# Padding in SBUF in a two-block fp32 kernel: where the tiles begin

## The chip, the cores and the metric

The kernel runs on one core of a Trainium2 chip. The metric is the device time of one launch in microseconds (us), the median of three runs. Nothing runs on the host but a re-layout of the inputs before the launch.

## The reference, cut to what matters

Two transformer blocks follow each other on 256 tokens of width 1024, all in float32. The first block has a SwiGLU feed-forward layer, a mixer and a second SwiGLU layer, the second block the same on 256 tokens plus 256 context tokens, with a modulation computed from a conditioning vector.

```python
def first_block(x, ...):
    x = x + 0.5 * swiglu(rmsnorm(x, ffn1_norm), w_gate, w_up, w_down)      # 1024 -> 2816 -> 1024
    x = x + hybrid_mixer(rmsnorm(x, mix_norm), w_in, ...)                  # gated linear attention and a short convolution
    x = x + 0.5 * swiglu(rmsnorm(x, ffn2_norm), ...)
    return rmsnorm(x, final_norm)

def second_block(x, c, ctx, ...):
    h, hc = x + grid_pos_emb(rows), ctx
    mods, mods_c = silu(c) @ w_ada + b_ada, silu(c_ctx) @ w_ada + b_ada    # nine vectors each
    h  = ffn_sublayer(h,  mods[0:3],   g_ffn1, w_ffn1_in, w_ffn1_out)
    hc = ffn_sublayer(hc, mods_c[0:3], g_ffn1, w_ffn1_in, w_ffn1_out)
    # mLSTM over both directions, a spatial gating branch, a merge and an output projection
    ...
    h  = ffn_sublayer(h, mods[6:9], g_ffn2, w_ffn2_in, w_ffn2_out)
    return rmsnorm_2(h, g_final)
```

## The kernel before, in words

Tokens are held in tiles of 128; a tile of activations is transposed by TensorE into XH and XL, so that the channel stands on the partitions. Almost every product of the kernel is done in three matmuls of type float32r: each fp32 operand is split into a rounded high part and the remainder (`split_out`: ScalarE copies the high part, VectorE subtracts it), and `mm3` or `mm3r` add high x high, high x low and low x high in one PSUM bank.

A weight comes as a unit of 128 x 1024 fp32 (512 KB): `load` issues its DMA on SyncE into one of 4 `raw` buffers, `split` writes it into one of 5 `wh` and one of 5 `wl` buffers. A matmul `mm(out, l, r)` loads `l` into the array (the stationary operand, an LDWEIGHTS of 128 columns) and streams `r` through it (the moving operand). In the profile's names, `acc<-wh,XH` is a matmul with moving wh and stationary XH.

- `proj_chunk` (gate and up layers of the two-token feed-forward layers, mixer projections): stationary XH or XL, moving wh or wl, 512 columns.
- `projT2` (gate and up layers of the second block): the other way round, stationary wh or wl, moving XH or XL, 512 columns for four token tiles and 256 for two.
- The down layers in `ffn2tok` and `ffn4tok`: stationary the hidden activations (high part hh, low part hl), moving wh or wl, 512 columns. The hidden tiles are taken by `salloc` from 18 shared buffers S0 to S17, the one that was freed longest ago first.

In `ffn4tok`, the first part of the down layer has six units for each half d of the output. A unit is 24 matmuls: two values of q, four token tiles, three products. In the built program the hidden pairs (hh, hl) of the six units stand in (S3, S4), (S7, S5), (S13, S14), (S16, S17), (S8, S9) and (S10, S11), the same for both values of d. With FFN4's first chunk, in `proj_chunk`, eight weight tiles that were split ahead into slots are the moving operands: (S1, S12), (S3, S11), (S2, S8), (S4, S7), for two token tiles one after the other, six matmuls for each pair and token tile.

The order of the work on each engine is that of the program text. SBUF is laid out pool by pool in the order of the pools in `body` and, within a pool, in the order in which tags first appear, each buffer rounded up to 32 bytes: const (with ident, mhalf, tri, XH, XL and others), xres, small, tmp, bc, rp, slots, raw, wsp. What stands where is therefore the running sum of the sizes before it. `salloc` asks for shapes up to 4096 bytes of the partition, and for two shapes of 4 x 258 elements (4128 bytes).

Of the kernel before, what the change touches and what calls it, by code (L numbers as in the profile page):

```python
# [9 lines left out]
F32 = mybir.dt.float32  # L10
F32R = mybir.dt.float32r
# [3 lines left out]
P = 128  # L15
D = 1024
# [7 lines left out]
class Kern:  # L24
# [26 lines left out]
    def psum(self, tag, shape):  # L51
        return self.ps.tile(shape, F32, tag=tag, name=self.nm(tag), bufs=4)

    def salloc(self, shape, dt=F32):
        i = self.free_slots.pop(0)
        t = self.slots.tile(shape, dt, tag=f"S{i}", name=self.nm(f"S{i}"))
        self.slot_of[id(t)] = (i, t)
        return t

# [1044 lines left out]
    def run(self):  # L1104
        nc, A = self.nc, self.A
        x = {}
        for t in (2, 3):
            x[t] = self.xres.tile([P, D], F32, tag=f"x{t}", name=f"x{t}")
        self.ident = self.cpool.tile([P, P], F32, tag="ident", name="ident")
        make_identity(nc, self.ident)  # L1110
        g = {"f1": self.bc.tile([P, D], F32, tag="bc", name="bc_f1")}
        pre = []
# [5 lines left out]
        self.mhalf = self.cpool.tile([P, 4], F32, tag="mhalf", name="mhalf")  # L1118
        nc.gpsimd.memset(self.mhalf, -0.5)
        self.tri = self.cpool.tile([P, 2, P], F32, tag="tri", name="tri")  # L1120
        self.XH = self.cpool.tile([P, 8, 512], F32R, tag="XH", name="XH")
        self.XL = self.cpool.tile([P, 8, 512], F32R, tag="XL", name="XL")
        lat = (2, 3)

        def res_half(t, d, ps):
# [173 lines left out]
def body(tc, A, out):  # L1299
    with tc.tile_pool(name="const", bufs=1) as cpool, \  # L1300
            tc.tile_pool(name="xres", bufs=1) as xres, \
            tc.tile_pool(name="small", bufs=16) as small, \
            tc.tile_pool(name="tmp", bufs=6) as tmp, \
            tc.tile_pool(name="bc", bufs=4) as bc, \
            tc.tile_pool(name="rp", bufs=2) as rp, \
            tc.tile_pool(name="slots", bufs=1) as slots, \
            tc.tile_pool(name="raw", bufs=4) as raw, \
            tc.tile_pool(name="wsp", bufs=5) as wsp, \
            tc.tile_pool(name="dram", bufs=1, space=bass.MemoryType.DRAM) as dram, \
            tc.tile_pool(name="ps", bufs=1, space=bass.MemoryType.PSUM) as ps:  # L1310
        pools = dict(cpool=cpool, xres=xres, small=small, tmp=tmp, bc=bc, rp=rp, slots=slots, raw=raw, wsp=wsp, ps=ps)
        k = Kern(tc, A, out, pools)
        k.modd = dram.tile([112, P], F32, tag="modd", name="modd")
        k.mrow = dram.tile([36, 256], F32, tag="mrow", name="mrow")
        k.run()
# [129 lines left out]
```

## Time and profile before

| | us |
|---|---|
| median of 3 runs | 1427.51 (1427.47 to 1428.04) |
| profiled execution, its own time | 1426.11 |
| its span, first to last instruction | 1424.3 |
| PE (matmuls) busy | 1404.2 (99%), 7222 instructions |
| PEld (weight loads) busy | 1170.0 (82%) |
| DVE (VectorE) busy | 919.5 (65%) |
| ACT (ScalarE) busy | 626.5 (44%) |

The granted clock of TensorE is 0.998 of full speed over the span. Matmuls are pipelined and the ends of their records are modelled, so a record's duration (393 ns and more for 512 columns) overlaps the next; what a matmul costs is the distance from its start to the next one's start. A distance is read from the timeline (start times of rows and the number of matmuls between them) or from a window, whose busy time is divided by the matmuls that start in it. A window's count has up to four more than that, since records that reach over its edges are counted too.

### The profile page before, as it was taken

What the parts mean: (1) busy time and instruction counts of PE and PEld (TensorE: products, weight loads), DVE (VectorE), ACT (ScalarE), POOL (GpSimd) and SP (SyncE); (2) the same over time, 40 slices, a digit from 0 to 9 for tenths busy, and PEclk for the clock granted to TensorE, in tenths of its full rate; (3) what the DMA queues carried; (4) which work ended last, traced back from release to release, by engine and by line L of the source; (5) the groups of instructions that cost most, each with busy time, mean ns of one, the idle gap of its engine ahead of it and who ended that gap; (6) DMA issues with size and microseconds to landing.
All of it is one profiled execution on the core that took longest, in us unless ns stands there. A gap on an engine that the chain in (4) does not pass through costs nothing. (4 is left out here: it accounts for less than half of the span.)

```text
span 1424.3 us, 18795 instructions
## 1 busy us (share of the span) xinstructions
PE 1404.2 (99%) x7222; PEld 1170.0 (82%) x7222; DVE 919.5 (65%) x1308; ACT 626.5 (44%) x914; POOL 29.3 (2%) x49
## 2 busy tenths in 40 slices
PE   7999999999999999999999999999999999999997
PEld 5888788778888898888888887888988887899986
DVE  5998556878988475542555446476886566655545
ACT  5445447464446442322122224343865455444442
POOL 0000000000000000000000001001010000000000
PEclk9999999999999999999999999999999999999999
DMA  8888646457887664643565442333335666465662
GB/s 278 307 269 275 205 136 204 134 166 259 290 275 254 203 210 132 195 147 102 191 209 178 147 148 94 115 104 129 102 104 187 198 192 206 142 197 179 184 207 69
DMA packets 73307, 260.71 MB, mean 183 GB/s; under 512 B 8172, under 2 KB 9216, under 8 KB 73216
## 3 DMA queue, kind: packets, MB, share of 16 engines
q1 hardware_dynamic: 72928, 259.11, 56.3%
q8 instruction: 57, 0.93, 0.3%
q10 hardware_dynamic: 288, 0.39, 0.1%
q14 instruction: 34, 0.28, 0.1%
HBM read 258.32 MB, written 1.14 MB: 182 GB/s over the span
## 5 line engine op out<-in xcount | busy, mean ns | idle before, releaser
L69 DVE TENSOR_TENSOR wl<-raw,wh 128x1024 fp32r<-128x1024 f32 (+1 forms) x381 | 459.0, 1212 | 330.3 <-ACT wh L66 326.7
L66 ACT ACTIVATE wh<-raw 128x1024 fp32r<-128x1024 f32 (+1 forms) x381 | 398.3, 1049 | 609.0 <-PE acc L79 457.9
L79 PE MATMUL acc<-wh,XH 128*128 128x512 f32 (+2 forms) x816 | 277.3, 398 | 0.4 <-ACT t L66 0.4
L79 PE MATMUL acc<-wh,XL 128*128 128x512 f32 (+2 forms) x816 | 273.4, 393 | 0.2 <-DVE XL L69 0.2
L79 PE MATMUL acc<-wl,XH 128*128 128x512 f32 (+2 forms) x816 | 272.4, 392 | 0.0
L79 PE MATMUL acc<-wh,S 128*128 128x512 f32 x872 | 237.1, 394 | 0.4 <-DVE t L72 0.4
L79 PE MATMUL acc<-XH,wh 128*128 128x512 f32 (+1 forms) x776 | 201.5, 339 | 0.0
L79 PE MATMUL acc<-XH,wl 128*128 128x512 f32 (+1 forms) x776 | 201.2, 339 | 0.0
L79 PE MATMUL acc<-XL,wh 128*128 128x512 f32 (+1 forms) x776 | 201.1, 339 | 0.0
L79 PEld LDWEIGHTS acc<-wh,S 128*128 128x128 f32 x872 | 162.8, 188 | 38.8 <-DVE t L72 1.1
L543 DVE SCALAR_TENSOR_TENSOR S<-raw,S 128x1024 f32<-128x1024 f32 x112 | 136.9, 1222 | 70.6 <-DMA raw<-in_w_ada 69.9
L79 PEld LDWEIGHTS acc<-wh,XL 128*128 128x128 f32 x816 | 152.2, 189 | 34.6 <-DVE XL L69 1.1
L79 PEld LDWEIGHTS acc<-wl,XH 128*128 128x128 f32 x816 | 152.0, 188 | 33.7 <-DVE wl L69 0.3
L79 PEld LDWEIGHTS acc<-wh,XH 128*128 128x128 f32 x816 | 151.7, 189 | 33.9 <-ACT t L66 0.6
L79 PEld LDWEIGHTS acc<-XL,wh 128*128 128x128 f32 x776 | 133.0, 188 | 17.5
L79 PEld LDWEIGHTS acc<-XH,wl 128*128 128x128 f32 x776 | 132.9, 188 | 17.5
L79 PEld LDWEIGHTS acc<-XH,wh 128*128 128x128 f32 x776 | 132.9, 188 | 17.5
L79 PE MATMUL acc<-wl,S 128*128 128x512 f32 x436 | 133.0, 393 | 0.0
L79 PEld LDWEIGHTS acc<-wl,S 128*128 128x128 f32 x436 | 81.9, 188 | 18.4
L66 ACT ACTIVATE S<-t 128x512 fp32r<-128x512 f32 (+2 forms) x58 | 31.4, 542 | 30.2 <-DVE t L69 30.2
L66 ACT ACTIVATE XH<-tr 128x512 fp32r<-128x512 f32 x44 | 26.0, 596 | 41.8 <-PE tr L152 41.3
L152 PE MATMUL tr<-ident,t 128*128 128x128 f32 x200 | 32.1, 285 | 10.4 <-DVE t L69 9.6
(165 smaller groups left out, 892.9 us busy)
## 6 DMA issues: line engine op xcount, KB each, us to landing
raw<-in_gu SPq DMA_DIRECT2D x176, 512.0 KB, 4.4
raw<-in_d SPq DMA_DIRECT2D x88, 512.0 KB, 4.3
raw<-in_w_ada SPq DMA_DIRECT2D x72, 512.0 KB, 4.5
raw<-in_w_in SPq DMA_DIRECT2D x68, 512.0 KB, 4.3
raw<-in_w_qk SPq DMA_DIRECT2D x16, 512.0 KB, 3.5
bc<-modd SPq DMA_DIRECT2D x10, 512.0 KB, 4.4
raw<-in_w_out SPq DMA_DIRECT2D x8, 512.0 KB, 3.5
raw<-in_w_b SPq DMA_DIRECT2D x8, 512.0 KB, 4.3
```

The lines of the kernel that those rows point to most:

```text
L66: return self.nc.scalar.activation(out=out, in_=in_, func=func, **kw)
L69: return self.nc.vector.tensor_tensor(out=out, in0=a, in1=b, op=op)
L79: self.nc.tensor.matmul(out, l, r, start=start, stop=stop, **kw)
L152: self.nc.tensor.transpose(tr[:, j, :], src[:, j * P:(j + 1) * P], self.ident)
L543: nc.vector.scalar_tensor_tensor(out=junk, in0=raw, scalar=1.0, in1=cb[r], op0=ALU.mult, op1=ALU.mult, accum_out=mc[:, o:o + 1])
```

## The change

One tile of 96 elements and one of 32 are added in the const pool and one of 96 in the rp pool; nothing writes or reads them. XH and XL move up in the const pool to stand right behind ident. `salloc` asks for 1152 elements in place of 4 x 258 and hands out the first 1032 of them in the old shape (the row of a head stays 258 elements, the buffer becomes 4608 bytes).

The instructions of all engines, their order and their waits are the same in both programs; apart from the row length of the 4 x 258 tiles only start addresses differ. In the built programs the starts within the partition, in bytes modulo 512, are:

```
                         before                          after
ident                    128                             0
XH, XL                   160                             0
x, tmp (t), bc           0                               0
S0 / S1                  128 / 160                       0 / 0
S2, S3                   192                             0
S4 to S7                 224                             0
S8 to S12                256                             0
S13 to S17               288                             0
raw, wh, wl              288                             0
tri                      160                             32
cst, mc, cols            160, 288, 224                   160, 288, 224
```

The pieces that the matmuls take from these tiles lie at multiples of 512 bytes from their starts, except in the 4 x 258 tiles, whose heads follow each other at 1032 bytes.

```diff
--- before.py
+++ after.py
+    def pad(self, pool, n):
+
+        pool.tile([P, n], F32, tag=f"pad{n}", name=self.nm("pad"), bufs=1)
+
     def salloc(self, shape, dt=F32):
         i = self.free_slots.pop(0)
-        t = self.slots.tile(shape, dt, tag=f"S{i}", name=self.nm(f"S{i}"))
+        if len(shape) == 3 and shape[1] * shape[2] > D:
+            t = self.slots.tile([P, D + P], dt, tag=f"S{i}", name=self.nm(f"S{i}"))
+            t = t[:, :shape[1] * shape[2]].rearrange("p (a b) -> p a b", a=shape[1])
+        else:
+            t = self.slots.tile(shape, dt, tag=f"S{i}", name=self.nm(f"S{i}"))
         self.slot_of[id(t)] = (i, t)
         return t
...
+        self.pad(self.cpool, 96)
         self.ident = self.cpool.tile([P, P], F32, tag="ident", name="ident")
+        self.XH = self.cpool.tile([P, 8, 512], F32R, tag="XH", name="XH")
+        self.XL = self.cpool.tile([P, 8, 512], F32R, tag="XL", name="XL")
...
         self.tri = self.cpool.tile([P, 2, P], F32, tag="tri", name="tri")
-        self.XH = self.cpool.tile([P, 8, 512], F32R, tag="XH", name="XH")
-        self.XL = self.cpool.tile([P, 8, 512], F32R, tag="XL", name="XL")
+        self.pad(self.cpool, 32)
...
         k = Kern(tc, A, out, pools)
+        k.pad(rp, 96)
```

## Rows read from the trace of the kernel before

**Rows 1.** Page, part 1: busy us, share of the span, instructions.
```profile
PE 1404.2 (99%) x7222; PEld 1170.0 (82%) x7222; DVE 919.5 (65%) x1308; ACT 626.5 (44%) x914; POOL 29.3 (2%) x49
```
**Rows 2.** Waits of PE, the longest: us in total, times, longest us.
```profile
PE tr L152 <- DVE t L69: 9.6, 3, 6.4
```
**Rows 3.** Groups by form, matmuls and a weight load: count, busy us, mean ns.
```profile
L79 PE MATMUL acc<-wh,XH 128*128 128x512 f32 x784 | 271.3, 402 | 0.4 <-ACT t L66 0.4
...
L79 PE MATMUL acc<-wh,S 128*128 128x512 f32 x872 | 237.1, 394 | 0.4 <-DVE t L72 0.4
L79 PEld LDWEIGHTS acc<-wh,S 128*128 128x128 f32 x872 | 162.8, 188 | 38.8 <-DVE t L72 1.1 <-ACT t L66 0.7 <-DVE t L69 0.5
...
L79 PE MATMUL acc<-wl,S 128*128 128x512 f32 x436 | 133.0, 393 | 0.0
...
L79 PE MATMUL acc<-XH,wh 128*128 128x512 f32 x392 | 123.8, 395 | 0.0
...
L79 PE MATMUL acc<-XH,wh 128*128 128x256 f32 x384 | 77.7, 282 | 0.0
```
**Rows 4.** Timeline of PE, ffn4tok's down layer, first rows of units: start, us, what.
```profile
652.45 2.00 PE L79 MATMUL acc<-wh,S 128*128 128x512 f32 x8
...
657.95 2.00 PE L79 MATMUL acc<-wh,S 128*128 128x512 f32 x8
...
663.41 1.98 PE L79 MATMUL acc<-wh,S 128*128 128x512 f32 x8
...
668.86 2.03 PE L79 MATMUL acc<-wh,S 128*128 128x512 f32 x8
...
674.46 0.39 PE L79 MATMUL acc<-wh,S 128*128 128x512 f32 x1
...
702.14 2.03 PE L79 MATMUL acc<-wh,S 128*128 128x512 f32 x8
...
707.74 0.39 PE L79 MATMUL acc<-wh,S 128*128 128x512 f32 x1
```
**Rows 5.** Windows, PE: us, busy (count), PEclk, DMA share, GB/s; XH with wh.
```profile
46.28:57.55 11.27, 11.27 (x52) 1.00 0.93 337
...
579.78:646.79 67.01, 67.01 (x291) 1.00 0.48 155
713.33:825.32 111.99, 111.99 (x481) 1.00 0.53 172
1097.95:1155.90 57.95, 57.95 (x253) 1.00 0.61 196
```
**Rows 6.** Timeline of PE, FFN4's first chunk, moving operands in slots.
```profile
1237.49 0.63 PE L79 MATMUL acc<-S,XH 128*128 128x512 f32 x2
...
1238.89 0.62 PE L79 MATMUL acc<-S,XH 128*128 128x512 f32 x2
...
1240.26 0.40 PE L79 MATMUL acc<-XH,wh 128*128 128x256 f32 x2
```
**Rows 7.** Windows of PE where all matmuls have 256 columns.
```profile
517.10:521.88 4.78, 4.78 (x43) 1.00 0.71 231
...
1246.31:1354.61 108.30, 108.30 (x915) 1.00 0.61 188
```
**Rows 8.** Groups by form of DVE and ACT.
```profile
L69 DVE TENSOR_TENSOR wl<-raw,wh 128x1024 fp32r<-128x1024 f32 x373 | 453.4, 1222 | 328.4 <-ACT wh L66 326.4 <-PE acc L79 1.0
...
L66 ACT ACTIVATE t<-x 128x512 f32<-128x512 f32 x31 | 19.4, 627 | 28.8 <-DVE x L72 20.4 <-DVE x L69 8.5
...
L66 ACT ACTIVATE t<-S 128x512 f32<-128x512 f32 x13 | 8.1, 622 | 2.9 <-DVE S L72 2.9
...
L72 DVE SCALAR_TENSOR_TENSOR bc<-bc,bc 128x1024 f32<-128x1024 f32 x3 | 3.7, 1224 | 1.5 <-DMA bc<-modd 1.5
```
**Rows 9.** Window, all engines: us, PE, PEld, DVE, ACT, POOL busy (count), PEclk, DMA.
```profile
50.00:100.00 50.00, 50.00 (x225) 40.43 (x224) 45.96 (x67) 23.96 (x30) 0.00 (x0) 1.00 0.86 285
```
**Rows 10.** Page, part 6: DMA issues, count, KB each, us to landing.
```profile
raw<-in_gu SPq DMA_DIRECT2D x176, 512.0 KB, 4.4
...
bc<-modd SPq DMA_DIRECT2D x10, 512.0 KB, 4.4
```

## The prediction

> **What bounds the kernel now.** I read the page first: PE is busy for 1404.2 of the 1424.3 us of the span, and no other engine for more than 65% of it [rows 1]. Then the waits of PE: the longest group that it waits for is 9.6 us in three waits, 6.4 us the longest [rows 2]. So there is next to no idle time to gain. The time is the number of matmuls times the distance between their starts, and the only way in which moved addresses can change it much is through that distance.
>
> The groups by form give the counts [rows 3]. Matmuls of 512 columns: three groups of 784 with a moving weight and XH or XL stationary (one of the three is shown), three of 392 the other way round (one shown), 872 + 436 with a stationary in the shared slots S, and 48 of FFN4's first chunk, 4884 in all. Those of 256 columns, nearly all between XH/XL and wh/wl, are about 1450. Durations in these rows can't be used, since they overlap. A weight load takes 188 ns [rows 3], so that for most of a matmul of 512 columns TensorE reads two things from SBUF: the moving rows of this matmul and the stationary rows of the next.
>
> The timeline then gives the distance, and a natural experiment: in ffn4tok's down layer the units are the same 24 matmuls in the same loop, and only the slots of the stationary differ [rows 4]. With moving wh and wl at 288 modulo 512:
> - pair (S7, S5), at 224: 657.95 - 652.45 = 5.50 us, 229.2 ns a matmul
> - (S13, S14), at 288: 663.41 - 657.95 = 5.46 us, 227.5 ns
> - (S16, S17), at 288: 668.86 - 663.41 = 5.45 us, 227.1 ns
> - (S8, S9), at 256: 674.46 - 668.86 = 5.60 us, 233.3 ns
>
> The second half of the output has the same pair (S8, S9) at 707.74 - 702.14 = 5.60 us again. So the distance depends on where the two operands begin. Written as the difference of the starts modulo 256, it is 227.3 ns for a difference of 0, 229.2 for 64 and 233.3 for 32.
>
> The bulk of the kernel has a difference of 128 (XH at 160 with wh at 288, either way round). There the windows give 11.27 us / 48 = 234.8 ns, 67.01 / 288 = 232.7, 111.99 / 480 = 233.3 and 57.95 / 249 = 232.7 [rows 5] (a chunk of proj_chunk and a step f of projT2 have 48 matmuls; the counts shown hold up to four records that reach over an edge, and 249 start inside the last). The clock is full in all of them, and their DMA shares go from 0.48 to 0.93 without an order in the distances of the last three. This bulk is as slow as the bad slots.
>
> **The change part by part.** After it all these tiles begin at multiples of 512, so every pair of operands of a float32r matmul, but for the 4 x 258 tiles, has a difference of 0 modulo 256. Nothing is added to any engine's queue: no instruction, wait or DMA is added or moved.
>
> - *Slots as stationary, 1308 matmuls.* By the slots that the built program uses, 412 have a difference of 0 already and gain nothing; 352 (S4 to S7) go from 229.2 to 227.3, 0.7 us; 518 (S2, S3, S8 to S12) go from 233.3 to 227.3, 3.1 us; 26 in S0 and S1 are worth 0.1 us. Sum 3.9 us. The moving slots of FFN4's first chunk, 24 of 48 in bad places, give 0.1 us.
> - *XH or XL against wh or wl, 3 x 784 + 3 x 392 = 3528 matmuls.* No row shows these loops at a difference of 0, so this is the term that is bounded and not read. At best they fall to the slots' 227.3: with 232.8 as their distance now (between the windows of 232.7 and 233.3, leaving out the slower 234.8), 5.5 ns x 3528 = 19.4 us. At worst 128 is as good as 0 and the loops are slow for another reason, such as two matmuls in a row on the same moving rows: 0 us. I take 228.3, a little above the slots, because these loops have sinks and transposes between them: 4.5 ns x 3528 = 15.9 us.
> - *256 columns, about 1450 matmuls.* Against slots at 256 (a difference of 160) 4.78 us / 40 = 119.5 ns, and against wh (a difference of 128) 108.30 / 912 = 118.8 ns [rows 7]. Two different offsets, one distance; a difference of 0 isn't shown. I take 0, with bounds of -2 ns (the step between a difference of 64 and 0 above) or 2.9 us gained, and +1 ns or 1.4 us lost.
> - *VectorE and ScalarE.* bc has begun at a multiple of 512 before, and VectorE takes 1224 ns over 1024 elements of it against 1222 ns for wl from raw and wh, all at 288. ScalarE takes 627 ns from x, aligned, against 622 ns from S [rows 8]. So 0, and it would lie beside PE anyway. Without that cover one per cent of VectorE's 919.5 us would be 9 us.
> - *DMA.* bc, aligned before, and raw, not aligned, both land in 4.4 us for 512 KB [rows 10]: 0, hidden under a full PE.
> - *What is late next.* Where VectorE is fullest, 45.96 of 50 us [rows 9], PE would run its share of work some 2% faster, which asks 94% of VectorE in place of 92%. That is close, but still below PE. Should VectorE bind in such stretches, some 190 us of feed-forward work, their part of the gain (190 x 2%, 3.8 us) is lost.
>
> Sum: 3.9 + 0.1 + 15.9 = 19.9 us. Against the profiled execution's own 1426.1 us this makes 1406.2; the median of the runs shown is 1.4 us above that execution, so 1427.5 - 19.9 = 1407.6, and I predict 1407.5 us.
>
> [...] [Rows 4] show the same 24 matmuls in 5.45 or 5.60 us by the slot that the weight load reads. [...]
>
> **The rivals.**
> - *Only the slots gain.* The bulk's 232.8 has another cause than its difference of 128. For it: the windows of the bulk differ by 2 ns at one and the same difference, so the loop counts too. Against it: the slots at 0 and 64 are both lower than any window of the bulk. Time: 1427.5 - 4.0 = 1423.5.
> - *No change.* The steps between the units come from something that goes with the slot's number and not with its address, or what one pair gains another loses. Against it: the same figure for (S8, S9) in both halves. Time: 1427.5, within 0.2%.
> - *Slower: a start at a multiple of 64 is what is slow.* The fast pairs (288 with 288, 288 with 224) have both starts at 32 modulo 64, the slow pair has a stationary at 0 modulo 64. FFN4's first chunk has XH at 160 stationary and the slots moving: six matmuls from S2 and S8, at 192 and 256, take 1238.89 - 1237.49 = 1.40 us, 233.3 ns; from S4 and S7, at 224, 1240.26 - 1238.89 = 1.37 us, 228.3 ns [rows 6]. So it is not the stationary alone, and a difference explains both loops; but no pair of float32r operands is at 0 modulo 64 on both sides, so the trace does not exclude that such a start costs by itself. Then all 4884 would take 233.3: 412 x 6.0 + 352 x 4.1 + 3528 x 0.5 = 5.7 us more, 1433.2. It decides from the first down layer on. Against it: two starts that are equal modulo 512 are the fastest that the trace has.
> - *More than forecast.* The bulk reaches 227.3 and the 256 columns gain 2 ns: 4.0 + 19.4 + 2.9 = 26.3 us, 1401.2; whole lines from their start could add a little to that.
>
> **How the numbers follow.** Forecast, between 1401 and 1414 (the bulk gains at least half of what I give it): 0.70. More than 26 us: 0.04. Only the slots, or little more, 1414 to 1424: 0.12. No change: 0.07. Slower: 0.07. The range 1398 to 1424 takes in the forecast, the slots alone and a few us beyond the best bound, 0.84 by these chances. A run of this kernel tells 0.2%, 2.9 us, from no change; the slots alone are just beyond that, so a part of their chance goes to the same: faster 0.82, same 0.11, slower 0.07.
>
> **What would show it.** In the changed kernel's timeline the six units of ffn4tok's down layer should all take 5.45 to 5.50 us, whatever their slots. The step f windows of projT2 (48 matmuls) should fall from 11.17 us to about 10.95, and the 256 column stretch should stay at 118.8 ns. VectorE's and ScalarE's means should stay within 1%, and PE should still wait for no more than now. It is wrong if the units become equal and projT2 stays at 232.7 (then the difference of 128 was no loss), if the units become equal at 233 (the slower rival), or if the distances fall and the time doesn't, with waits of PE on VectorE in their place.

## The result, and the profile after

The changed kernel takes 1410.1 us (median of 4 runs, 1408.26 to 1413.17) against 1427.49 us (4 runs, 1427.29 to 1428.04): a ratio of 0.988, 95% interval 0.986 to 0.990. 1407.5 us was forecast. The profiled executions are 1408.26 and 1426.11 us, 17.85 us apart; the comparison below is of these two.

Part 1 of the changed kernel's page answers to [rows 1]:

```profile
PE 1384.6 (98%) x7222; PEld 1169.7 (83%) x7222; DVE 919.1 (65%) x1308; ACT 627.3 (45%) x914; POOL 30.4 (2%) x49
```

The waits of PE answer to [rows 2] (us in total, times, longest):

```profile
PE tr L160 <- DVE t L77: 9.4, 3, 6.9
PE acc L87 <- DVE wl L77: 1.3, 3, 0.8
```

The same instructions, the same busy time of VectorE and ScalarE, and 19.6 us less of PE. The second wait is new; more on it below.

The timeline of PE in ffn4tok's down layer answers to [rows 4]: the same units, now all equal.

```profile
643.64 1.98 PE L87 MATMUL acc<-wh,S 128*128 128x512 f32 x8
...
649.09 1.98 PE L87 MATMUL acc<-wh,S 128*128 128x512 f32 x8
...
654.52 1.98 PE L87 MATMUL acc<-wh,S 128*128 128x512 f32 x8
...
659.97 1.98 PE L87 MATMUL acc<-wh,S 128*128 128x512 f32 x8
...
665.40 0.39 PE L87 MATMUL acc<-wh,S 128*128 128x512 f32 x1
...
692.81 1.98 PE L87 MATMUL acc<-wh,S 128*128 128x512 f32 x8
...
698.25 0.39 PE L87 MATMUL acc<-wh,S 128*128 128x512 f32 x1
```

The reader sees 5.45, 5.43, 5.45, 5.43 and 5.44 us for 24 matmuls, 226.2 to 227.1 ns each; (S8, S9), from 659.97 to 665.40 and from 692.81 to 698.25, no longer differs from the others.

The windows of PE where XH and XL meet wh and wl answer to [rows 5], those of 256 columns to [rows 7] (us, busy and count, granted clock, DMA share, GB/s):

```profile
44.65:55.65 11.00, 11.00 (x51) 1.00 0.93 309
56.01:68.26 12.25, 11.93 (x52) 1.00 0.83 267
572.60:637.99 65.39, 65.39 (x290) 1.00 0.51 159
703.69:812.49 108.80, 108.80 (x481) 1.00 0.55 179
1081.85:1138.41 56.56, 56.56 (x252) 1.00 0.61 200
...
510.77:515.64 4.87, 4.87 (x43) 1.00 0.65 217
1227.83:1337.35 109.52, 109.52 (x915) 1.00 0.61 187
```

With 48, 288, 480 and 249 matmuls: 229.2 ns (234.8 before), 227.0 (232.7), 226.7 (233.3) and 227.1 (232.7). At 256 columns it goes the other way, 109.52 / 912 = 120.1 ns against 118.8, and 4.87 / 40 = 121.8 against 119.5. The second window, a chunk of the first feed-forward layer with the same 48 matmuls as the one above it, takes 12.25 us: PE waits in it.

Summed over the timeline, from each start to the next: the 3528 matmuls between XH/XL and wh/wl take 819.1 us in place of 833.7, waits included (-14.6), those with a stationary in the slots 300.5 in place of 305.0 (-4.5), those of 256 columns 168.0 in place of 166.3 (+1.7); the rest is within 1 us. Counting only distances under 260 ns, the 3528 gain 19.2 us; the other 4.6 us go to longer gaps.

### The profile page after: what moved, and what is told of

Its sections match the earlier page's. It is cut to its first block, busy times and chain, and to the rows that moved or that the text cites. A ratio compares the mean times of both kernels' runs of the same rounds, so it can differ in the third digit from the quotient of the medians.

```text
span 1406.5 us, 18795 instructions
## 1 busy us (share of the span) xinstructions
PE 1384.6 (98%) x7222; PEld 1169.7 (83%) x7222; DVE 919.1 (65%) x1308; ACT 627.3 (45%) x914; POOL 30.4 (2%) x49
## 5 line engine op out<-in xcount | busy, mean ns | idle before, releaser
L87 PE MATMUL acc<-wh,XH 128*128 128x512 f32 (+2 forms) x816 | 273.6, 393 | 0.5 <-ACT t L74 0.4
L87 PE MATMUL acc<-wl,XH 128*128 128x512 f32 (+2 forms) x816 | 268.9, 388 | 1.5 <-DVE wl L77 1.3
L87 PE MATMUL acc<-wh,XL 128*128 128x512 f32 (+2 forms) x816 | 269.5, 388 | 0.2 <-DVE XL L77 0.2
L87 PE MATMUL acc<-wh,S 128*128 128x512 f32 x872 | 234.2, 391 | 0.2 <-DVE t L80 0.2
L551 DVE SCALAR_TENSOR_TENSOR S<-raw,S 128x1024 f32<-128x1024 f32 x112 | 136.8, 1222 | 68.8 <-DMA raw<-in_w_ada 67.9
L160 PE MATMUL tr<-ident,t 128*128 128x128 f32 x200 | 32.1, 285 | 10.5 <-DVE t L77 9.4
```

The lines of the kernel that those rows point to most:

```text
L87: self.nc.tensor.matmul(out, l, r, start=start, stop=stop, **kw)
L160: self.nc.tensor.transpose(tr[:, j, :], src[:, j * P:(j + 1) * P], self.ident)
L551: nc.vector.scalar_tensor_tensor(out=junk, in0=raw, scalar=1.0, in1=cb[r], op0=ALU.mult, op1=ALU.mult, accum_out=mc[:, o:o + 1])
```

## Experiments

They ask what in the addresses counts (1, 2), where the new waits come from (3), and what a better placement gives (4). Distances quoted without a window are means over the distances below 260 ns from one start to the next, read from the timeline and grouped by the difference of the moving start and the next stationary start, modulo 256.

### 1. All tiles 32 bytes higher

```diff
-        self.pad(self.cpool, 96)
+        self.pad(self.cpool, 104)
```

> All tiles stand 32 bytes higher than in the changed kernel: XH, XL, all slots, raw, wh and wl at 32 modulo 512, so that no operand begins at a multiple of 64, and every difference of moving and stationary start is still 0. Theory A (only the difference of the two starts counts): 227 ns a matmul of 512 columns everywhere, 120.0 ns at 256 columns, a time as that of the changed kernel, 1408 to 1413 us. Rival B (a start at a multiple of 64 or 512 is what gains): back to 229 to 233 ns, 1418 to 1427 us. Rival C (starts at a multiple of 64 cost something, hidden in the gain): under 227 ns, below 1405 us.

Measured 1410.98 us, ratio to before 0.9887 (0.9870 to 0.9903), that of the change itself. The windows of PE (gate and up of the second block with XH moving, projections of the second block's mixer with XH stationary, 256 columns) are those of the changed kernel to 0.01 us:

```profile
574.50:639.90 65.40, 65.40 (x291) 1.00 0.52 160
1083.80:1140.36 56.56, 56.56 (x252) 1.00 0.61 198
1230.18:1339.69 109.51, 109.51 (x915) 1.00 0.61 187
```

No operand of these loops begins at a multiple of 64, and nothing is lost. The multiples of 512 do nothing by themselves; that the two operands begin alike modulo 256 is enough (0 and 32 modulo 512 are the two places tried; experiment 4 tells 256 from 512). Rivals B and C fall; the slower rival of the prediction fell with the result.

### 2. XH and XL at 128, 64, 32 and 16, all else at multiples of 512

The edit for 128 (a second pad keeps what follows in its place); 64, 32 and 16 alike, the last by a slice from the 4th element of a wider tile:

```diff
         self.ident = self.cpool.tile([P, P], F32, tag="ident", name="ident")
+        self.pad(self.cpool, 32)
         self.XH = self.cpool.tile([P, 8, 512], F32R, tag="XH", name="XH")
...
-        self.pad(self.cpool, 32)
+        self.pad(self.cpool, 128)
```

> As the changed kernel, but XH and XL begin at 128 modulo 512; slots, wh and wl stay at 0. Theory A: the 3528 matmuls of 512 columns between XH/XL and wh/wl go back to 232.5 to 234.8 ns as before the change, the slots stay at 227.3, and the matmuls of 256 columns go from 120.0 back to 118.7 ns: 1410 + 3528 x 5.5 ns - 1448 x 1.3 ns = about 1427 less the waits in the first feed-forward layer that come with the faster matmuls, 1422 to 1427 us. Rival B (multiples of 128 are good enough, both ends on whole lines): 227 ns everywhere and 1408 to 1413 us.

> As the changed kernel, but XH and XL begin at 64 modulo 512. Theory A, by the slots before the change (a difference of 64: 229.2 ns): 3528 matmuls at about 229.2 in place of 227.3, 6.7 us more than the changed kernel, some 1415 to 1418 us; the sign of the difference (wh minus XH in the projections, XH minus wh in the second block's gate and up layers) should not matter. At 256 columns 118.7 to 120 ns, not known. Rival B: 227 ns and 1408 to 1413 us.

> As the changed kernel, but XH and XL begin at 32 modulo 512. Theory A, by the slots before the change (a difference of 32: 233.3 ns): 3528 matmuls at 233.3 in place of 227.3, some 1424 to 1429 us. Rival B (every start off a multiple of 64 costs the same): between this and the run at 64, no lower than it.

> As the changed kernel, but XH and XL begin at 16 modulo 256. Theory A: the distance is set by the difference, and 16 lies between 0 and 32: somewhere from 227 to 233 ns for the 3528 matmuls, not the same for the two signs, 1410 to 1425 us; at 256 columns with XH moving 116.8 to 120 ns. Rival (only multiples of 32 matter): as the changed kernel, 227 and 120.0 ns.

Measured: at 128 1423.51 us, ratio 0.9974 (0.9963 to 0.9984); at 64 1419.24 us, at 32 1423.69 us and at 16 1418.55 us (one run each, beside 1427.4 and 1427.5 us of before). The same three windows of PE with XH at 128:

```profile
579.00:646.02 67.02, 67.02 (x291) 1.00 0.50 155
1095.86:1153.81 57.95, 57.95 (x252) 1.00 0.61 194
1244.32:1352.62 108.30, 108.30 (x915) 1.00 0.63 188
```

with XH at 64:

```profile
577.85:643.86 66.01, 66.01 (x291) 1.00 0.50 159
1091.44:1149.63 58.19, 58.19 (x252) 1.00 0.60 193
1240.81:1348.31 107.50, 107.50 (x916) 1.00 0.62 190
```

and with XH at 32:

```profile
580.33:647.60 67.27, 67.27 (x290) 1.00 0.49 154
1097.53:1155.71 58.18, 58.18 (x252) 1.00 0.59 195
1246.24:1352.74 106.50, 106.50 (x916) 1.00 0.63 193
```

and with XH at 16, with a later stretch of 128 matmuls of the same kind as the second row between the two last:

```profile
576.81:643.62 66.81, 66.81 (x291) 1.00 0.50 157
1092.08:1148.61 56.53, 56.53 (x252) 1.00 0.62 200
1154.97:1184.95 29.98, 29.98 (x131) 1.00 0.60 193
1239.39:1347.70 108.31, 108.31 (x916) 1.00 0.63 188
```

At 128 all three windows have gone back to the 67.01, 57.95 and 108.30 us of [rows 5] and [rows 7], and the 3.9 us that are left are the slots' gain. So the bulk was slow because of its difference of 128, which no row of before could show. At 64 the two directions differ, against what was expected: with XH moving (moving minus stationary is 64) 66.01 / 288 = 229.2 ns, with XH stationary (minus 64) 58.19 / 249 = 233.7. This is why that run came out at 1419 and not at 1415 to 1418. But the sign is not all: a later projection with XH moving, 216 matmuls in the same order and with the same difference of 64, takes 50.49 / 216 = 233.8 ns:

```profile
923.68:974.17 50.49, 50.49 (x218) 1.00 0.32 106
```

At 32 both signs are at 233.6 ns; the run is just under its 1424 to 1429 us, since the 256 columns, which that sum left out, gain there too. At 16 the expected range holds, but one and the same difference gives 56.53 / 249 = 227.0 ns in one stretch and 29.98 / 128 = 234.2, as slow as before the change, in a later one; over all, the distances scatter from 227 to 235 ns (231.7 and 231.1 on average). So equal starts give the short distance in all windows of 512 columns taken in the second block (226.7 to 227.1 ns), while at 16 and 64 something besides the difference counts, and no run here shows what.

| moving minus stationary, mod 256 | 0 | 16 | 32 | 64 | 96 | 128 | 192 | 224 | 240 |
|---|---|---|---|---|---|---|---|---|---|
| 512 columns, ns | 227 | 231.7 | 233.3 | 229.7 | 233.7 | 232.8 | 233.3 | 233.3 | 231.1 |
| 256 columns, ns | 120.1 | 118.8 | 116.8 | 117.9 | | 118.8 | | | |

(96 is from the slots before the change, the others from the changed kernel and the four runs; 16, 64 and 240 are means of loops that differ, as above. The second row is the last window of each run, divided by its 912 matmuls.) At 256 columns the order is another: 0 is the worst value seen and 32 the best.

### 3. The new waits in the first feed-forward layer

In the changed kernel the chunks of this layer take 11.00, 12.25, 11.22, 11.00, 12.09, 11.43, 11.60 and 11.00 us, where they took 11.24 to 11.38 before: 3.6 us over eight times 11.00. The eight take 91.6 us in all, 1.3 us more than before, although their matmuls are faster. My first theory was that DMA, at 0.93 and 309 GB/s in the first chunk, had become the limit there.

```diff
-            self.fill_every = 2 if self.filler is not None and 1 <= c < 10 else 0
+            self.fill_every = every if self.filler is not None and 1 <= c < 10 else 0
...
-                self.fill_every = 1 if f0 + 4 < f or f0 else 0
+                self.fill_every = 1 if f0 + 1 < f or f0 else 0
...
-        self.ffn2tok(A["gu1"], A["d1"], xts, rows, res_half, after)
+        self.ffn2tok(A["gu1"], A["d1"], xts, rows, res_half, after, every=3)
```

> The changed kernel, but the modulation weights (512 KB each) come after every third instead of every second weight unit in the first feed-forward layer; the six that are left over come earlier in the second block's gate and up layers. Theory A: the new waits of PE in the first layer (chunks of 12.25, 12.09, 11.60 us beside others of 11.0) are waits for DMA, which at 290 to 310 GB/s is full there once the matmuls are faster. With less to load they go: about 3.5 us less, 1406 to 1407.5 us, and the runs lie within 1.5 us instead of 5. Rival B: VectorE, 92 to 95% busy there, is what binds; it has six times 2.4 us less work there too, so the time alone would not tell, but then ScalarE would no longer be seen to wait for raw before the late splits. Rival C: the waits come from the order of the queues and stay: 1408 to 1413 us.

> The kernel before with that same move of six modulation units. Theory A: with the slower matmuls DMA kept up, so there is little to win: 1425 to 1428 us, at most 1.5 us less than before. Rival: if it gains 3 us or more, the waits in the first layer have nothing to do with the change.

Measured: 1407.07 us, ratio 0.9860 (0.9847 to 0.9874), and for the kernel before with the same edit 1426.86 us, ratio 0.9995 (0.9986 to 1.0004). The chunks are all at 11.00 to 11.02 us again, so the waits go, and before the change there were none to remove. The scatter of the runs stays (1406.28 to 1410.73 us), against what was expected, and of the 4 us won in this layer 2.0 us are lost again between 505 and 528 us, where the second block's first matmuls of 256 columns wait for the normalised tiles (waits of PE of 0.9 us for t and 0.7 us for XL, both from VectorE; in the changed kernel it has none there). This edit takes work from DMA and VectorE alike, so two more runs take it from one alone, in ada_gen:

```diff
-                    nc.vector.scalar_tensor_tensor(out=junk, in0=raw, scalar=1.0, in1=cb[r], op0=ALU.mult,
-                                                   op1=ALU.mult, accum_out=mc[:, o:o + 1])
+                    nc.vector.scalar_tensor_tensor(out=junk[:, :128], in0=raw[:, :128], scalar=1.0, in1=cb[r][:, :128],
+                                                   op0=ALU.mult, op1=ALU.mult, accum_out=mc[:, o:o + 1])
```

> The changed kernel with the product of the modulation cut to the first 128 of 1024 columns of each weight (it leaves out 7/8 of that sum), while its DMA stays whole: VectorE has about 1 us less work per modulation unit and vector, the DMA the same. Theory A (DMA is what the first feed-forward layer waits for): its chunks stay uneven, between 11.0 and 12.3 us, with 3 to 5 us of waits in all from 45 to 145 us; 1406 to 1412 us. Rival B (VectorE): all chunks 11.0 to 11.05 us.

```diff
-                nc.sync.dma_start(out=raw, in_=A["w_ada"][mods[0] * 8 + q])
+                nc.sync.dma_start(out=raw[:, :512], in_=A["w_ada"][mods[0] * 8 + q][:, :512])
...
+                    for half in (0, 512):
+                        nc.vector.scalar_tensor_tensor(out=junk[:, :512], in0=raw[:, :512], scalar=1.0,
+                                                       in1=cb[r][:, half:half + 512], op0=ALU.mult, op1=ALU.mult,
+                                                       accum_out=mc[:, o:o + 1])
```

> The changed kernel with half of each modulation weight loaded (256 in place of 512 KB; it uses the first half in place of the second), while VectorE does two products of 512 columns in place of one of 1024, 1.38 us against 1.22. Theory A: with half the extra DMA all chunks of the first feed-forward layer take 11.0 to 11.05 us, 1405 to 1408 us, although VectorE has more to do. Rival B (VectorE): the waits stay or grow, 1409 to 1414 us.

Measured 1404.7 us with less on VectorE and 1415.04 us with less on DMA, a little over rival B's range (two runs each). Theory A falls, VectorE it is. Windows of all engines in this layer (us, then PE, PEld, DVE, ACT, POOL busy with counts, clock, DMA share, GB/s), first of the run with the products cut:

```profile
56.28:67.30 11.02, 11.02 (x52) 9.05 (x51) 7.30 (x15) 5.35 (x7) 0.00 (x0) 1.00 0.83 282
90.38:101.38 11.00, 11.00 (x52) 9.05 (x50) 6.24 (x15) 4.65 (x7) 0.00 (x0) 1.00 0.89 313
```

and of the run with half the DMA:

```profile
55.99:68.04 12.05, 11.38 (x51) 8.84 (x49) 10.73 (x22) 5.46 (x7) 0.00 (x0) 1.00 0.65 201
68.40:80.75 12.35, 11.68 (x52) 8.80 (x51) 10.91 (x22) 5.46 (x7) 0.00 (x0) 1.00 0.63 203
```

The chunk runs at 11.00 us with DMA at 0.89 and 313 GB/s, and waits with DMA at 0.63 when VectorE has more to do. The waits of the weight load name it too. From 45 to 140 us, in the kernel before:

```profile
PEld acc L79 <- DVE wl L69: 0.3, 1, 0.3
```

in the changed kernel:

```profile
PEld acc L87 <- DVE wl L77: 3.9, 6, 1.2
```

and with half the DMA (with the products cut there is none):

```profile
PEld acc L87 <- DVE wl L77: 8.7, 13, 1.1
```

What had misled me was ScalarE, which waits 47.7 us for raw in this stretch (44.9 us in the kernel before). But SyncE issues the load of raw only when VectorE has given the buffer back, as its own waits in the changed kernel, from 45 to 140 us, show:

```profile
SPq L108 <- DVE S L551: 33.1, 15, 3.3
SPq L108 <- DVE wl L77: 24.4, 21, 2.4
SPq L548 <- DVE wl L77: 16.4, 13, 2.4
```

In the kernel before, these three are 33.0, 24.5 and 15.9 us: they show who gives the buffers back, not what is new. Nor are faster matmuls needed for the new waits. With XH at 32 a chunk without a wait takes 11.28 us, no less than before, and yet its eight chunks take 92.6 us, with this wait of the weight load from 45 to 140 us:

```profile
PEld acc L87 <- DVE wl L77: 3.1, 5, 1.1
```

So the waits hang on VectorE's work, as the two runs above show; what sets them off after the change and not before it, with one profile of each kernel, stays open. A nearly full engine alone does not set them off: in the second SwiGLU layer of the changed kernel a chunk takes 11.00 us with VectorE busy for 10.55 of them and DMA at 0.97 and 364 GB/s.

```profile
370.40:381.40 11.00, 11.00 (x51) 9.06 (x50) 10.55 (x14) 5.47 (x7) 0.00 (x0) 1.00 0.97 364
```

### 4. A better version: 256 columns at a difference of 32

wh and wl get 1088 columns, and where 256 columns are used (FFN4 from its third hidden block on, and q in the mixer) they begin at the 56th element, 224 bytes:

```diff
-            wh = self.wsp.tile([P, 1024], F32R, tag="wh", name=self.nm("wh"))
-            wl = self.wsp.tile([P, 1024], F32R, tag="wl", name=self.nm("wl"))
+            wh = self.wsp.tile([P, 1088], F32R, tag="wh", name=self.nm("wh"))[:, self.at:self.at + 1024]
+            wl = self.wsp.tile([P, 1088], F32R, tag="wl", name=self.nm("wl"))[:, self.at:self.at + 1024]
...
+            self.at = 56
             for f in range(2, NF):
...
+            self.at = 0
```

> The changed kernel, but where a projection of the second block runs on 256 columns (feed-forward 2 from its third hidden block on, and q) wh and wl begin at 224 modulo 256, so that the moving XH minus the stationary is 32. Theory A: these 1152 matmuls take 116.8 ns, as with XH at 32, in place of 120.0: 3.7 us less than the changed kernel, 1405 to 1409 us, while those of 512 columns stay at 227. Rival B (the shorter distance at 256 columns came from XH's place and not from the difference): 120.0 ns and 1408 to 1413 us.

> The changed kernel with both edits, fewer modulation units in the first feed-forward layer and wh and wl at 224 modulo 256 where 256 columns are used. Theory A: the gains add, 3.7 us of the 256 columns and 2 to 3 us of the waits: 1402 to 1405 us. Rival: the waits come back at another place, 1405 to 1407 us.

Measured 1405.61 us, ratio 0.9848 (0.9834 to 0.9861), and with the edit of the modulation units as well 1403.91 us, ratio 0.9840 (0.9821 to 0.9859; 5 runs, 1402.36 to 1408.94). The windows of PE in the first of the two:

```profile
575.51:640.91 65.40, 65.40 (x291) 1.00 0.50 160
1230.54:1337.03 106.49, 106.49 (x916) 1.00 0.63 193
```

106.49 / 912 = 116.8 ns, with 512 columns still at 227.1: among the differences tried each of the two loops has its own best one, and the two can be had together. In this kernel neighbouring wh buffers, and wl buffers, stand 4352 bytes apart, so that at 512 columns some differences are 0 and some 256 modulo 512. Both give 226.7 ns where XH moves (628 and 543 distances) and 227.6 and 227.4 where it is stationary: what counts is the difference modulo 256. The last version is 23.8 us under the kernel before, run beside it at 1427.70, and some 6 us under the changed kernel; that it is faster than the one with the first edit alone is not shown, since their intervals overlap.

## Why the prediction was right, point by point

- *The distance is set by where the operands begin* [rows 4]: right at 512 columns, and with equal starts it is as short at 32 as at 0 modulo 512 (65.40 and 65.39 us for 288 matmuls, 227.1 and 227.0 ns; experiment 1). By other differences it is not fixed alone: 64 gave 229.2 and 233.8 ns, -16 gave 227.0 and 234.2 (experiment 2). What makes these steps of up to 7 ns a matmul, no run shows. Nor does the trace of before settle whether a matmul's own stationary counts or the next one's: with the differences of the built program's slots, the step from 0 to 32 takes 234.7 ns and back 229.7, but from 0 to 64 it takes 227.6 and back 231.5 (22 to 31 distances each).
- *Slots, 3.9 us:* right. With XH put back to a difference of 128 the gain is 3.9 us, in the medians; the timeline of the changed kernel gives 4.5.
- *The bulk, 15.9 us:* the cause, the difference of the starts, was right and the term too small. The distances fell to 226.7 to 227.1 where 228.3 was taken, in windows from 232.7 and 233.3; over all 3528 the gain is 19.2 us, the best bound of 19.4 and not the middle. My reason for the middle, sinks and transposes between the matmuls, was wrong: these cost the same before and after (the 200 transposes `tr<-ident,t` of one line: 32.1 us busy in both; all matmuls outside the three sums above: within 1 us). The rival that only the slots gain falls with it.
- *256 columns, 0:* wrong in sign and outside its bounds. I had two offsets with one distance and took the loop for insensitive; a difference of 0 costs 1.3 ns there, 1.7 us in all.
- *What is late next:* left out of the sum, and only the engine and the place were right. VectorE holds up the first feed-forward layer by 3.6 us. That this is near the 3.8 that the prediction named is luck: those were the whole gain of both layers, while one layer lost 3.6, more than its gain, and the second none. Nor was it the faster PE alone, as the prediction had it, since the slow matmuls of XH at 32 wait too. The busy share did not tell: 94% was taken for enough, and the second SwiGLU layer, as full (10.55 of 11.00 us in a chunk), has no such waits.
- *VectorE, ScalarE, DMA at 0:* right. wl from raw and wh takes 1222 ns as before, x in ScalarE 629 (627), raw lands in 4.3 us (4.4) [rows 8, 10].
- *The signs that it set:* the units at 5.43 to 5.45 us, projT2's step at 65.39 / 6 = 10.90 us and the means of VectorE and ScalarE came as said. Two did not: the 256 columns left 118.8 ns, and PE waits for VectorE where it had not.
- *The sum:* 4.5 + 19.2 - 1.7 - 3.6 = 18.4 us, against 17.85 between the profiled executions and 19.9 forecast. That the time came out near is in part luck: the bulk's term was too small, and two losses that the sum put at 0 balance it.

## What to carry to other kernels

Where TensorE is full, look at the distance between matmul starts, not at the busy share (99% before, 98% after), and compare the same loop on different buffers: the difference that followed the slots here was one of addresses, since the units took 5.43 to 5.45 us whatever their slots once the starts were equal. Place moving and stationary operands relative to each other and try the difference for each loop: of those tried here 0 was best at 512 columns (227 ns) and 32 at 256 columns (116.8 ns, against 120.1 at 0). When PE gets faster by 2%, add up the busy time per chunk of whoever feeds it; over 90% was no margin in one layer here, which lost 3.6 us, while another, with VectorE at 96% in a chunk, lost nothing. And look behind a wait "for DMA": the 47.7 us that ScalarE waited for raw here had buffers behind them that VectorE gave back late (SyncE waited 33.1, 24.4 and 16.4 us for it).

## What the runs showed of the hardware that was not expected

- The distance of float32r matmuls of 512 columns goes from 227 to 234 ns with the difference of the operands' starts modulo 256, shortest at 0. The place of equal starts did not matter where it was tried: 0 and 32 modulo 512 gave the same to 0.01 us in a window of 65 us.
- At other differences a loop can have two distances: 229.2 and 233.8 ns at 64, 227.0 and 234.2 at -16, each within one run.
- At 256 columns the order is another: 120.1 ns at 0, 116.8 at 32.
- With equal starts the distances become regular: of the distances below 270 ns between matmuls of 512 columns (some 4,690 in each kernel), 89% are 226 or 227 ns in the changed kernel, 8% in the one before.
